# Four tiny reads on 15, 14, 8 and 7 DMA engines, late in a fused add and layer norm

## The chip, the cores and the metric

The kernel runs on one core of one Trainium2 chip. The metric is the device time of the run in microseconds (us). The kernel before takes 239.56 us (median of two runs, 239.42 to 239.70). Where a profile is quoted, the span on it (238.4 us) is a little shorter than the device time of the same run (239.69 us).

## The reference, cut to what matters

```python
# x, residual: 16 x 1024 x 512 float32; gamma, beta: 512
z = x + residual
mean = np.mean(z, axis=-1, keepdims=True)
var = np.var(z, axis=-1, keepdims=True)
z_norm = (z - mean) / np.sqrt(var + eps)
return (gamma * z_norm + beta).astype(np.float32)
```

That is 67.11 MB to read and 33.55 MB to write, with very little arithmetic for each byte.

## The kernel before

All large transfers are issued by SP, the sync engine, in one fixed order, and are carried out by 16 DMA engines (each large transfer has 16 landings in the trace). The trace does not number the engines. "Engine" with a number is a label of this document, for the order in which small transfers reach them: engine 15 is the one that 15 rows leave out. The general-purpose engine POOL adds, the scalar engine ACT makes the mean and the variance, the vector engine DVE normalizes in place in `zbuf`, and SP stores from `zbuf`. Each of the 128 partitions has room for 64 rows in `zbuf` and 32 in `rbuf`, so loads late in the list wait until a store has freed its rows. In this cut some lines of bookkeeping are left out, and the comments are added.

```python
X_CHUNKS = [8] * 15 + [4, 4]          # rows of a partition in each load
R_CHUNKS = [8] * 15 + [4, 4]
OUT_CHUNKS = [16] * 7 + [8, 4, 4]     # rows of a partition in each store
Z_ROWS, R_ROWS, STORE_LAG = 64, 32, 40
...
for c, (lo, n) in enumerate(loads_x):
    asked = lo + n
    while stored < asked - Z_ROWS:                     # room in zbuf?
        o = next(i for i, b in enumerate(stores) if b[0] == stored)
        nc.sync.wait_ge(so[o], 16)
        stored += stores[o][1]
    move(part(zbuf, Z_ROWS, lo, n), dram(xf, lo, n), sx[c])
    while todo_r and ...:
        wait_rows(s_add, "add", rlo + rn - R_ROWS)
        move(part(rbuf, R_ROWS, rlo, rn), dram(rf, rlo, rn), sr[rc])
    while todo_o and ...:
        wait_rows(s_out, "out", olo + on)
        move(dram(of, olo, on), part(zbuf, Z_ROWS, olo, on), so[oc])
for o, (lo, n) in enumerate(stores[:-1]):              # the end of the run
    if lo >= stored:
        nc.sync.wait_ge(so[o], 16)
nc.sync.sem_clear(range(nums[0], nums[-1]))
nc.sync.wait_ge(so[-1], 16)
```

Chunks are counted from 0 below. A load of 8 rows is 2 MB and puts 16 KB on each partition; a store of 16 rows is 4 MB and 32 KB.

## Time and profile before

| | before |
|---|---|
| device time | 239.56 us |
| transfers busy, share of 16 engines | 99.1% |
| ACT, DVE, POOL busy | 78%, 74%, 60% |
| last store landed | 238.33 us of a span of 238.4 us |

These are lines of the profile's page of the kernel before. The digits are busy tenths in 40 equal slices, and the line of queue 1 gives packets, MB and share of the time of 16 engines.

```profile
span 238.4 us, 1803 instructions
PE 3.7 (2%) x4; PEld 1.2 (0%) x4; DVE 177.2 (74%) x290; ACT 186.5 (78%) x545; POOL 142.2 (60%) x21
...
DMA  8999999999999999999999999999999999999996
...
DMA packets 6340, 100.67 MB, mean 422 GB/s; under 512 B 706, under 2 KB 706, under 8 KB 708
...
q1 hardware_dynamic: 6336, 100.67, 99.1%
...
ACT 38%; DMA 33%; issue 10%; POOL 7%; ACTq 5%; DVE 3%; SPq 1%; DVEq 0%; POOLq 0%
```

The transfers are full from the second slice to the last but one. The last line is the chain of waits; it runs through ACT for 38% of the span, but ACT is busy for only 78% of it, while the transfers have no idle slice. The reading is that the transfers bound this kernel.

The change is placed in the stretch around 142 us, so here are SP's issues there in the kernel before, from the timeline of SP (start, duration, what it issues).

```profile
141.22 0.43 SPq L138 DMA_DIRECT2D zbuf<-in_x_dram  x1
141.70 0.43 SPq L138 DMA_DIRECT2D rbuf<-in_residual_dram  x1
169.39 0.33 SPq L138 DMA_DIRECT2D zbuf<-in_x_dram  x1
```

SP issues x chunk 13 and residual chunk 13, and then x chunk 14 only 27 us later, when a store has freed rows. Meanwhile the engines work through what is queued. The end of the run shows in the waits of SP's own queue (line, what it waited for, total us, times, longest us):

```profile
SPq L166 <- DMA out_dram<-zbuf: 4.6, 2, 2.4
SPq L169 <- DMA out_dram<-zbuf: 2.3, 1, 2.3
```

These two lines are the wait for the stores after the last issue at 230.8 us.

One more reading is needed, and the page does not have it: the trace records when each of the up to 16 engines of a transfer reports that its part has landed. The following is worked out from those records of the kernel before; "late" is the last landing less the median one.

```
transfer            first     last      late
residual chunk 4     51.02     51.48    0.21
x chunk 9           114.39    115.25    0.63
residual chunk 13   177.74    179.14    1.13
last store          236.15    238.33    1.91
```

One landing falls behind the others, and only where stores run. It ends 1.5 us after the second last engine, so it alone sets the end of the run.

### The profile page before, as it was taken

Reading aid. Unit: us, or ns where it says so; the run is one execution under the profiler, and the core shown is the slowest. Engines: PE = TensorE matmul, PEld = TensorE weight load, DVE = VectorE, ACT = ScalarE, POOL = GpSimd, SP = SyncE. Lnnn points to the kernel's source line nnn. Section 1 sums busy time; section 2 is a strip of 40 time slices with the busy share of each in tenths; the row PEclk is TensorE's granted clock in tenths of the full one; section 3 lists DMA queues with packets and bytes.
Section 4 is the critical chain, followed back from the end, with each engine's and each line's share of the span. In section 5 each row is a group of like instructions: output and inputs, shape, how many; then the busy total and the mean of one; then the engine's idle time right before and its main releaser. Section 6 shows DMA issues by size and latency. Waiting matters only on the chain.

```text
span 238.4 us, 1803 instructions
## 1 busy us (share of the span) xinstructions
PE 3.7 (2%) x4; PEld 1.2 (0%) x4; DVE 177.2 (74%) x290; ACT 186.5 (78%) x545; POOL 142.2 (60%) x21
## 2 busy tenths in 40 slices
PE   0600000000000000000000000000000000000000
PEld 0100000000000000000000000000000000000000
DVE  0000488888888889998888888887888648888870
ACT  2003999999999999999999999989997399999700
POOL 0098988989889407893088930889209892770000
DMA  8999999999999999999999999999999999999996
GB/s 308 438 429 415 437 437 429 426 423 437 429 429 418 440 434 426 459 434 396 429 429 429 434 429 429 426 470 434 390 434 418 434 440 408 472 434 434 390 425 257
DMA packets 6340, 100.67 MB, mean 422 GB/s; under 512 B 706, under 2 KB 706, under 8 KB 708
## 3 DMA queue, kind: packets, MB, share of 16 engines
q1 hardware_dynamic: 6336, 100.67, 99.1%
q10 hardware_dynamic: 4, 0.00, 0.0%
HBM read 67.11 MB, written 33.55 MB: 422 GB/s over the span
## 4 chain that ended last, share of the span: by engine, by line
ACT 38%; DMA 33%; issue 10%; POOL 7%; ACTq 5%; DVE 3%; SPq 1%; DVEq 0%; POOLq 0%
DMA rbuf<-in_residual_dram 21%; ACT junk_s L203 20%; ACT junk_m L194 18%; DMA out_dram<-zbuf 12%; POOL zbuf L181 7%; ACTq L194 2%; DVE zbuf L228 2%; DVE zbuf L243 1%; ACTq L203 1%; SPq L138 1%; ACTq L189 1%; ACT std L211 0%; ACTq L201 0%; ACTq L210 0%; DVEq L228 0%
## 5 line engine op out<-in xcount | busy, mean ns | idle before, releaser
L181 POOL TENSOR_TENSOR zbuf<-zbuf,rbuf 128x4096 f32<-128x4096 f32 (+1 forms) x17 | 142.0, 8353 | 70.9 <-DMA rbuf<-in_residual_dram 70.9
L228 DVE SCALAR_TENSOR_TENSOR zbuf<-zbuf,nm,gamma_p 128x512 f32 x128 | 87.1, 743 | 50.4 <-ACT junk_s L203 50.4
L194 ACT ACTIVATE junk_m<-zbuf 128x512 f32 x128 | 74.9, 585 | 28.5 <-POOL zbuf L181 23.3
L203 ACT ACTIVATE junk_s<-zbuf,nm 128x512 f32 x128 | 88.8, 694 | 3.9
L243 DVE SCALAR_TENSOR_TENSOR zbuf<-zbuf,rstd,beta_p 128x512 f32 x128 | 87.1, 744 | 1.1
L203 ACT ACTIVATION_READ_ACCUMULATOR junk_s<-zbuf,nm x128 | 23.9, 187 | 0.0
L194 ACT ACTIVATION_READ_ACCUMULATOR junk_m<-zbuf x128 | 23.9, 187 | 0.0
L211 ACT ACTIVATE std<-ssq,eps_t x32 | 9.5, 297 | 3.7
L237 DVE RECIPROCAL rstd<-std x32 | 5.4, 170 | 0.0
L187 ACT ACT_TABLE_LOAD x1 | 1.3, 1283 | 2.7 <-PEq L55 2.7
L123 PE MATMUL gamma_p<-gb_row,ones 1*128 1x512 f32 x2 | 2.0, 1122 | 7.3 <-DMA gb_row<-in_gamma_dram 7.3
L123 PE MATMUL beta_p<-gb_row,ones 1*128 1x512 f32 x2 | 1.9, 1056 | 0.0
L118 DVE MEMSET ones<- 1x128 f32 x1 | 0.2, 165 | 2.0 <-PEq L55 2.0
L123 PEld LDWEIGHTS beta_p<-gb_row,ones 1*128 1x128 f32 x2 | 0.7, 332 | 1.0 <-DMA gb_row<-in_beta_dram 0.5
L123 PEld LDWEIGHTS gamma_p<-gb_row,ones 1*128 1x128 f32 x2 | 0.5, 305 | 7.3 <-issue 7.3
L278 POOL MEMSET const-float32-0.0<- 128x1 f32 x1 | 0.1, 99 | 0.2 <-issue 0.2
L278 POOL MEMSET const-bfloat16-1.0<- 128x1 bf16 x1 | 0.1, 101 | 0.0
L278 POOL MEMSET const-uint8-127<- 128x1 uint8 x1 | 0.1, 101 | 0.0
L278 POOL MEMSET const-float32-1.0<- 128x1 f32 x1 | 0.1, 98 | 0.0
L119 DVE MEMSET eps_t<- 128x1 f32 x1 | 0.1, 59 | 0.0
## 6 DMA issues: line engine op xcount, KB each, us to landing
zbuf<-in_x_dram SPq DMA_DIRECT2D x15, 2048.0 KB, 32.8
rbuf<-in_residual_dram SPq DMA_DIRECT2D x15, 2048.0 KB, 30.1
out_dram<-zbuf SPq DMA_DIRECT2D x7, 4096.0 KB, 28.6
zbuf<-in_x_dram SPq DMA_DIRECT2D x2, 1024.0 KB, 32.6
rbuf<-in_residual_dram SPq DMA_DIRECT2D x2, 1024.0 KB, 34.6
out_dram<-zbuf SPq DMA_DIRECT2D x1, 2048.0 KB, 15.0
out_dram<-zbuf SPq DMA_DIRECT2D x2, 1024.0 KB, 9.4
gb_row<-in_gamma_dram ACTq DMA_DIRECT2D x1, 2.0 KB
```

The costliest lines, as they stand in the source:

```text
L123: nc.tensor.matmul(dest[:, :], ones[:, :], gb_row[:, k * D : (k + 1) * D], start=True, stop=True).then_inc(s_pe, 1)
L138: i = nc.sync.dma_start(out=out, in_=in_).then_inc(s, 16)
L181: nc.gpsimd.tensor_tensor(out=z, in0=z, in1=part(rbuf, R_ROWS, a, an), op=ALU.add).then_inc(s_add, an)
L187: act.preload_act_table_set("sqrt_and_others")
L189: with act.Fori(0, turns) as t:
L194: act.activation(out=junk_m[k][:, :], in_=zbuf[:, bass.ds(zoff + k * D, D)], func=ACT.Identity, scale=-inv_d, accum_out=nm[:, bass.ds(r0 + ...
L203: act.activation(out=junk_s[k][:, :], in_=zbuf[:, bass.ds(zoff + k * D, D)], func=ACT.Square, bias=nm[:, bass.ds(r0 + k, 1)], accum_out=ss ...
L211: act.activation(out=std[:, bass.ds(r0, TURN)], in_=ssq[:, bass.ds(r0, TURN)], func=ACT.Sqrt, bias=eps_t[:, 0:1], scale=inv_d,).then_inc(s ...
L228: dve.scalar_tensor_tensor(out=row, in0=row, scalar=nm[:, bass.ds(r0 + k, 1)], in1=gamma_p[:, :], op0=ALU.add, op1=ALU.mult,)
L237: dve.reciprocal(out=rstd[:, bass.ds(r0, TURN)], in_=std[:, bass.ds(r0, TURN)]).then_inc(s_dve, TURN)
L243: dve.scalar_tensor_tensor(out=row, in0=row, scalar=rstd[:, bass.ds(r0 + k, 1)], in1=beta_p[:, :], op0=ALU.mult, op1=ALU.add,).then_inc(s_ ...
L278: nc = _bacc.Bacc("TRN2", target_bir_lowering=False, num_devices=1)
```

## The change

Four small reads are put on SP's queue just before the wait for x chunk 14. Nothing reads what they bring. They have 15, 14, 8 and 7 rows, of 64, 96, 128 and 160 bytes, and SP waits for them after all stores are issued. The sizes tell them apart in a trace, and the row counts tell engines apart: the intent is a label, not speed.

```diff
+PROBES = [(15, 16), (14, 24), (8, 32), (7, 40)]
...
+    probe = nc.alloc_sbuf_tensor("probe", [16, 128], FP32)
...
+    s_probe = [sem(f"probe{i}") for i in range(len(PROBES))]
...
     for c, (lo, n) in enumerate(loads_x):
         asked = lo + n
+        if c == len(loads_x) - 3:
+            at = 0
+            for i, (e, w) in enumerate(PROBES):
+                nc.sync.dma_start(out=probe[:e, at : at + w], in_=xf[:e, :w]).then_inc(
+                    s_probe[i], 16
+                )
+                at += w
         while stored < asked - Z_ROWS:
...
+    for s in s_probe:
+        nc.sync.wait_ge(s, 16)
     for o, (lo, n) in enumerate(stores[:-1]):
```

## The prediction

> **What bounds the kernel now.** The transfers. The DMA queue table gives queue 1 99.1% of sixteen engines' span (100.67 MB, mean 422 GB/s); ACT is busy 78%, DVE 74%, POOL 60%. The table by stages shows a DMA share of 0.99 to 1.02 from 20 us to 225 us. The chain of waits runs through ACT for long stretches, but it alternates with DMA there, and ACT has slack. So the time is bytes over rate, plus the tail: the last store lands at 238.3 us of a 238.4 us span.
>
> The landing times of each transfer, sixteen each, say more. Fifteen engines finish within about 0.6 us of each other; one falls behind. The spread from first to last landing grows from 0.45 us before the first store to 1.4 us at 179 us and 2.18 us at the end. It grows with the 4 MB stores, about 0.28 us each: that engine's 32 KB store packets take about 1,240 ns against 1,213 ns. This engine alone sets the end.
>
> **What the change does.** Four reads of 15x64 B, 14x96 B, 8x128 B and 7x160 B, issued before x chunk 14. Nothing else moves.[...] So engine 15 gets no probe, 14 one, 8 to 13 two, 7 three, 0 to 6 four. They look like labels that tell which engine lags.
>
> **Cost.**
> - Issue: 0.43 us each on SP's queue, as its neighbours, 1.9 us with gaps. They follow the residual issue at 141.70 us, and SP then waits for a store until 169.39 us. Off the path by 25 us.
> - Engines: a 4 B semaphore packet took 9 ns, a 2 KB packet 84 ns. I estimate 25 to 40 ns for a probe packet with its semaphore: at most 0.16 us on engines 0 to 6, 0.12 us on 7, 0 on 15. Fifteen engines have over 1.4 us of slack, so only what falls on the laggard counts.
> - Waits at the end: four satisfied semaphore waits, after the last issue at 230.8 us and under the last store's landing of 7.5 us. Zero.
> - 512 B more of SBUF per partition, four semaphores: zero.
>
> On the path: 0 if the laggard is engine 15, about 0.1 us if 7 or lower.[...] The trace before doesn't number the engines.[...]
>
> **Predicted time** 239.6 us; 239.1 to 240.2 should hold it 8 times in 10. Faster by over 2%: 0.01; within 2%: 0.98; slower by over 2%: 0.01.
>
> **What would show it.** The probes' issues appear at 142.1 to 144 us, about 0.43 us each, and x chunk 14 still issues at about 169.4 us. They land at 177.8 to 179.3 us, behind the residual chunk. If engine 15 lags, no probe has the landing that is late by about 1 us; if 7, the first three have it and the fourth not. 44 more data and 44 more semaphore packets. The last transfer's spread stays at 1.9 to 2.3 us. ACT, DVE, POOL busy times unchanged to 0.5%.
>
> **What would make it wrong.** A small descriptor that stalls the lagging engine[...]; a probe changing which engine is served first for the rest of the run; a transfer on fewer than 16 engines costing SP far more than 0.43 us; drift between runs over 0.3%.

The sum came to 239.6 us: 239.56 us of the kernel before, nothing for the issue, the waits and the space, and 0 or about 0.1 us for the probes on the lagging engine.

## The result, and the profile after

The changed kernel took 239.74 us (239.71 to 239.76, two runs) against 239.56 us. The ratio is 1.0009, with a 95% interval from 0.9985 to 1.0033. More rounds, on another occasion, are the first experiment below.

The same lines of the page, after:

```profile
span 238.4 us, 1809 instructions
PE 3.7 (2%) x4; PEld 1.2 (0%) x4; DVE 177.2 (74%) x290; ACT 186.5 (78%) x545; POOL 142.2 (60%) x21
...
DMA  8999999999999999999999999999999999999995
...
DMA packets 6428, 100.67 MB, mean 422 GB/s; under 512 B 794, under 2 KB 794, under 8 KB 796
...
q1 hardware_dynamic: 6424, 100.67, 99.1%
...
ACT 38%; DMA 33%; issue 10%; POOL 7%; ACTq 5%; DVE 3%; SPq 1%; DVEq 0%; POOLq 0%
```

The packets rise by 88: 15 + 14 + 8 + 7 = 44 rows and as many completions. (A completion is the packet of 4 bytes, of 9 ns, that goes with the landing of an engine's part of a transfer: there are 707 of them before and 751 after, 44 more for 44 more such landings.) The rest is the same. The issues of SP in the timeline, and its waits at the end:

```profile
141.16 0.43 SPq L143 DMA_DIRECT2D zbuf<-in_x_dram  x1
141.64 0.43 SPq L143 DMA_DIRECT2D rbuf<-in_residual_dram  x1
142.11 1.53 SPq L153 DMA_DIRECT2D probe<-in_x_dram  x4
169.33 0.36 SPq L143 DMA_DIRECT2D zbuf<-in_x_dram  x1
```

```profile
SPq L180 <- DMA out_dram<-zbuf: 4.6, 2, 2.4
SPq L183 <- DMA out_dram<-zbuf: 2.3, 1, 2.3
```

The four issues took 1.53 us in a gap of 27 us, x chunk 14 went out when it did before, and the added waits do not appear: the probes had landed 50 us earlier.

The landings of the four probes, worked out from the trace's records, are the interesting part. The first entry of each comes alone, 0.47 to 0.61 us after its issue, and no 4-byte packet goes with it (48 entries more than before, 44 packets more); the large transfers, with their 16 landings, have no such entry. What writes it was not shown. Then there is one for each row.

```
residual chunk 13   177.7 ... 178.2 178.3                                179.10
15 rows    142.7 |  177.9 ... 178.4 178.5                                179.31
14 rows    143.2 |  178.1 ... 178.6 178.7                                179.50
8 rows     143.5 |  178.3 178.4 178.5 178.6 178.6 178.6 178.9            179.68
7 rows     143.8 |  178.5 178.6 178.7 178.8 178.8 178.8                  179.88
```

That is 15, 14, 8 and 7 landings. The packets show which of the probes share an engine. In order of time the 44 packets fall into 15 series with steps of 13 to 16 ns, and each series starts with a packet of the first probe: seven have all four sizes, one has the first three, six the first two, and one the first alone. So the engines of a shorter probe are a part of those of a longer one, and the labels follow: engines 0 to 6 have all four probes, 7 has three, 8 to 13 have two, 14 has one and 15 none. (For fewer than seven rows it is taken for granted that the order goes on; there only the late engine was followed.) The late engine, which is in all four rows, is thus one of the engines 0 to 6. It is neither 15 nor 7.

The second thing to see is the spacing. The late engine ran its four probe packets in 0.06 us (178.61 to 178.67 us; 11 to 14 ns for each packet and 9 ns for each completion, overlapping a little). But their landings are 0.19 us apart, on this engine as on others. That is 0.77 us for four completions, twelve times the packets' time, and none of it reached the end of the run: the last store landed at 238.39 us, against 238.33.

### The profile page after: what moved, and what is told of

It is laid out like the page before. It is cut to its first block, busy times and chain, and to the rows that moved or that the text cites. A ratio compares the mean times of both kernels' runs of the same rounds, so it can differ in the third digit from the quotient of the medians.

```text
span 238.4 us, 1809 instructions
## 1 busy us (share of the span) xinstructions
PE 3.7 (2%) x4; PEld 1.2 (0%) x4; DVE 177.2 (74%) x290; ACT 186.5 (78%) x545; POOL 142.2 (60%) x21
## 4 chain that ended last, share of the span: by engine, by line
ACT 38%; DMA 33%; issue 10%; POOL 7%; ACTq 5%; DVE 3%; SPq 1%; DVEq 0%; POOLq 0%
DMA rbuf<-in_residual_dram 21%; ACT junk_s L217 20%; ACT junk_m L208 18%; DMA out_dram<-zbuf 12%; POOL zbuf L195 7%; ACTq L208 2%; DVE zbuf L242 2%; DVE zbuf L257 1%; ACTq L217 1%; SPq L143 1%; ACTq L203 1%; ACT std L225 0%; ACTq L215 0%; ACTq L224 0%; DVEq L242 0%
```

## The experiments

The rounds ran on three chips. Kernels of one call shared one chip and its runs of the kernel before, and every ratio is taken within such a call.

### The changed kernel again

Edit: none.

> The changed kernel itself, in more rounds. Theory (only what the probes add to the lagging engine counts; four probe packets with their semaphore packets took 0.06 us there): ratio 1.0003, between 0.9995 and 1.0012. Rival (the 0.18 us between the medians of the first two runs is a real cost, paid somewhere else than on the lagging engine): 1.0008 or more with an interval that leaves 1.0003 out. The lagging engine again lands last on all four probes if the lag belongs to one engine of the chip.

Measured: 239.65 us (239.55 to 239.67, five runs) against 239.65 us of before; ratio 0.9997, interval 0.9984 to 1.0011. What follows: the 0.18 us between the first medians is not a cost that can be told from nothing. The lagging engine was again in all four probes (its landings came at 179.12, 179.31, 179.50 and 179.70 us).

### Which engine lags

```diff
-PROBES = [(15, 16), (14, 24), (8, 32), (7, 40)]
+PROBES = [(6, 16), (5, 24), (4, 32), (3, 40), (2, 48), (1, 56)]
```

(The probe buffer was widened to fit.)

> Probes of 6, 5, 4, 3, 2 and 1 rows instead of 15, 14, 8 and 7, to find which of the engines 0 to 6 lags. If it is engine j, the probes of more than j rows have a landing about 0.8 us or more behind the others, and those of j rows or fewer have not. Time as before within 0.3%.

Measured: 239.76 us in one run of unknown state. The last landings:

```
6 rows: 179.35 (the one before it 178.3)      3 rows: 178.85
5 rows: 179.54 (the one before it 178.5)      2 rows: 179.04
4 rows: 178.69 (the one before it 178.7)      1 row:  179.22
```

What follows: the probes of 6 and 5 rows have a landing 1.0 us behind the others, and that of 4 rows has not. The lagging engine is the one that five rows reach and four do not, engine 4. Six small transfers on engine 0 and two on engine 4 cost nothing that shows.

### Twelve times as many

```diff
-PROBES = [(15, 16), (14, 24), (8, 32), (7, 40)]
+PROBES = [(15, 16), (14, 24), (8, 32), (7, 40)] * 12
```

(The destinations were spread over partitions so that they fit and do not overlap.)

> The four probes twelve times, 48 small transfers, issued in the same idle time of SP (about 20 us of issue from 142 us on, done before 169 us). Theory (a probe costs its packet times on the lagging engine and nothing else: 0.06 us for four): twelve times 0.06 = 0.7 us more, ratio 1.003 (1.002 to 1.004), and the lagging engine's distance to the median engine in the landing of the x chunk behind the probes not changed by more than 0.2 us, since the others carry nearly as many. Rival 1 (a small transfer stalls an engine[...], about 0.2 us each as the landings of the four are spaced): 48 x 0.2 = 9.6 us, ratio 1.04. Rival 2 (the cost is hidden altogether): 1.000.

Measured: 249.80 us; ratio 1.0416, interval 1.0402 to 1.0430, 10 us more. The first rival gave the right number. But two things happened in this run, as the timeline of SP and the stretches of the windows view show (in the latter: stretch, its length, busy us and instructions of PE, PEld, DVE, ACT and POOL, granted clock, DMA share, GB/s):

```profile
142.21 39.41 SPq L154 DMA_DIRECT2D probe<-in_x_dram  x48
181.67 0.36 SPq L143 DMA_DIRECT2D zbuf<-in_x_dram  x1
```

```profile
170.00:180.00 10.00, 0.00 (x0) 0.00 (x0) 8.67 (x15) 9.29 (x29) 0.47 (x1) 1.00 0.87 323
180.00:190.00 10.00, 0.00 (x0) 0.00 (x0) 8.26 (x13) 4.77 (x15) 8.38 (x1) 1.00 0.78 228
```

First, SP could not issue 48 transfers in 20 us. The first twelve went out within 4.5 us, and from then until about 176 us most took 1.2 us and four took 2.4 to 2.8, so x chunk 14 was issued at 181.67 us and not at 169.3. Even its first landing came 6.2 us later than before. Secondly, the engines lost unequal time: the last landing of x chunk 14 came 9.1 us later than before. So the match with 48 x 0.2 us was partly a coincidence, and the next kernels were made to separate the two.

### Waiting at once

```diff
                 at += w
+            for s in s_probe:
+                nc.sync.wait_ge(s, 16)
...
-    for s in s_probe:
-        nc.sync.wait_ge(s, 16)
```

> The same four probes, but SP waits for them directly after their issue, not at the end. Theory (the change is free because its wait stands behind the last issue): x chunk 14 is then issued at about 179.9 us, not 169.3 us, after the queue has run dry at 177.7 to 178.7 us; [...]an idle stretch of 3 to 4 us on every engine, and the time rises by 3 to 4 us, ratio 1.012 to 1.018. Rival (there is slack elsewhere that takes it up, since ACT and DVE have a backlog): within 0.3%.

Measured: 243.42 us; ratio 1.0152, interval 1.0136 to 1.0167, as expected. The wait of SP's queue, its timeline, and the DMA line of the view of transfers for 176 to 190 us (40 slices of 0.35 us):

```profile
SPq L158 <- DMA probe<-in_x_dram: 36.2, 1, 36.2
```

```profile
142.05 1.53 SPq L153 DMA_DIRECT2D probe<-in_x_dram  x4
179.92 0.36 SPq L143 DMA_DIRECT2D zbuf<-in_x_dram  x1
```

```profile
DMA  9995110000000093766898999979898996989999
```

What follows: x chunk 14 is issued 10.5 us later than before, and the queue runs dry for about 3.5 us. Data moves again in the slice from 180.9 us, 1.0 to 1.3 us after that issue. The change is free on SP's side because of where its waits stand. The slip of 10.5 us cost only 3.8 us, because the queue held most of the rest. While it was dry the late engine also caught up: at the end its landing is 0.80 us behind the median one, in place of 1.91.

### Sixteen in one burst

```diff
-PROBES = [(15, 16), (14, 24), (8, 32), (7, 40)]
+PROBES = [(15, 16), (14, 24), (8, 32), (7, 40)] * 4
```

> The four probes four times, 16 small transfers in one burst, issued by about 151 us, so that x chunk 14 is still issued at 169.4 us (in the run with 48 it slipped to 181.7 us, as SP's issue stretched to 1.2 us each after the 13th). Theory (an engine runs small packets at 16 ns each[...] and only their landings are spaced by 0.19 us): 16 x 0.016 = 0.25 us more, ratio 1.001. Rival (only about four can be outstanding, the others hold up the engine 0.19 us each): 12 x 0.19 = 2.3 us more, ratio 1.0095.

Measured: 242.58 us; ratio 1.0118, interval 1.0103 to 1.0134. The theory fell. The rival's 2.3 us were found on the lagging engine, but the interval leaves out its ratio of 1.0095. SP's timeline and the stretch from 177 to 182 us, first of this run and then, for comparison, of the kernel before:

```profile
142.09 9.34 SPq L154 DMA_DIRECT2D probe<-in_x_dram  x16
169.37 0.36 SPq L143 DMA_DIRECT2D zbuf<-in_x_dram  x1
...
177.00:182.00 5.00, 0.00 (x0) 0.00 (x0) 4.90 (x9) 4.70 (x14) 2.56 (x1) 1.00 1.04 318
```

```profile
177.00:182.00 5.00, 0.00 (x0) 0.00 (x0) 4.86 (x9) 4.69 (x14) 2.70 (x1) 1.00 1.00 426
```

Here x chunk 14 is issued on time, so SP is out of it. The DMA share still reads full, but only 318 GB/s move in place of 426. The busy share counts packets that are held up: behind the probes the trace has 16 KB packets of 0.7 to 2.4 us, where 0.61 is usual. From the last landing of residual chunk 13 to that of x chunk 14, the lagging engine took 7.18 us (179.29 to 186.47), against 4.89 us before (179.14 to 184.03). That is 2.29 us more, or twelve times 0.19 us. The first landing of x chunk 14 also came 0.46 us later, but that is another engine's: the landings that the probes of 15 and 14 rows lack put engines 15 and 14, with four probes or none, at about 178.2 us for residual chunk 13, and 4.89 us later is 183.1, where the first two landings stand (183.09 and 183.11). So those two were not slowed. At the end of the trace the last landing is 2.43 us later than before. Most of the rest of the measured 3.1 us lies outside the span that the profile shows: the device time exceeds the span by 1.8 us in all four runs of this kernel and by about 1.3 us in those of the others. Why was not found.

### Heavy reads on four engines or five

```diff
-PROBES = [(15, 16), (14, 24), (8, 32), (7, 40)]
+PROBES = [(4, 1024)] * 8          # the other kernel: (5, 1024)
...
+                    in_=xf[: 2 * e, :].rearrange("(p j) d -> p (j d)", j=2),
```

> Eight probes of four rows of 4 KB: about 0.165 us each, 1.3 us together, on engines 0 to 3 only. Theory (engine 4 alone sets the end, the others finish 1.5 us or more before it): ratio 1.000, within 0.0012; last landing of the run not moved. Rival (the mean load of the engines, or any engine's load, counts): 1.3 us, ratio 1.0055, or a part of it.

(The 0.165 us for a row is an estimate. In the trace before a packet of 2 KB takes 84 ns, one of 8 KB 309 ns and a completion 9 ns.)

Measured, four rows: 241.22 us; ratio 1.0071, interval 1.0058 to 1.0083.

> The same eight probes with five rows, so that engine 4, the lagging one, gets them as well. Theory: its 1.3 us go to the end in full, ratio 1.0055 (1.004 to 1.007), against 1.000 of the kernel with four rows. Rival (the lagging engine does not matter more than another): the same as with four rows, or a quarter more.

Measured, five rows: 242.92 us; ratio 1.0134, interval 1.0119 to 1.0149. The stretch of the run with four rows:

```profile
177.00:182.00 5.00, 0.00 (x0) 0.00 (x0) 4.96 (x9) 4.70 (x14) 1.47 (x1) 1.00 1.01 292
```

What follows: the first expectation missed. Only 292 GB/s moved in this stretch, more than half of its 16 KB packets took 0.7 to 1.25 us, and even the first landing of x chunk 14 came 1.5 us later than before. The heavy reads disturb engines that they do not use, so this pair is no clean test. All eight read the same 16 KB of x (20 KB with five rows), which may be the reason; that is argued and not shown. The difference of the two kernels, 0.0063 or 1.5 us, is near the 1.3 us expected for engine 4 alone. Each probe of five rows has one landing 1.8 to 2.7 us behind its next, those of four rows have none more than 0.36 us behind, so on this chip, too, engine 4 lags. A cleaner pair comes last.

### Stores in smaller pieces

```diff
-            move(dram(of, olo, on), part(zbuf, Z_ROWS, olo, on), so[oc])
+            for a in range(olo, olo + on, PIECE):          # PIECE = 8
+                an = min(PIECE, on)
+                move(dram(of, a, an), part(zbuf, Z_ROWS, a, an), so[oc])
```

(The waits for a store count 16 for each piece. This kernel has no probes.)

> No probes: the kernel before with every store cut into pieces of 8 rows, 16 KB per partition rather than 32 KB, issued at the same points. In the trace before, the lag of engine 4 grew by 0.25 us per 4 MB store with 32 KB packets and by 0.03 us in the 2 MB store with 16 KB packets. Theory (the lag comes with packets of 32 KB): the last landing is then 0.6 to 0.9 us behind the median one rather than 1.9, and the time falls by about 1.2 us, ratio 0.995. Rival (the lag comes with the bytes stored by this engine): lag and time unchanged, ratio 1.000 within 0.0015.

Measured: 240.06 us; ratio 1.0021, interval 1.0007 to 1.0034. The last store landed with its slowest engine 2.20 us behind the median one, against 1.91 before. What follows: the theory fell. The lag grew in small packets as in large ones, so shorter packets do not cure it; that it goes with the bytes stored fits, but was not tested by itself. Why engine 4 stores more slowly stays open.

### Twelve bursts of four

```diff
-        if c == len(loads_x) - 3:
+        if c >= 5:                       # four of the 48 probes before each chunk
+            for i, (e, w) in list(enumerate(PROBES))[4 * (c - 5) : 4 * (c - 4)]:
```

> The 48 small reads of the run at 249.8 us, but as twelve bursts of four, one before each of the last twelve x chunks, so that 5 us or more of ordinary transfers lie between two bursts. Theory (an engine's completions of small transfers land 0.19 us apart, but the engine runs up to about 0.8 us ahead of them, so a burst of four is hidden and each further one in the same burst costs 0.19 us): 12 x 0.06 = 0.7 us at most, ratio 1.000 to 1.004. Rival 1 (each small transfer costs 0.19 us wherever it stands, less the first four): 44 x 0.19 = 8.4 us, ratio 1.035. Rival 2 (a part of every burst shows): in between, 1.01 to 1.03.

Measured: 241.85 us; ratio 1.0090, interval 1.0076 to 1.0104. That is 2.2 us for 48 small transfers, where the single burst took 10.2 us. The theory expected at most 0.7 us, so the direction is right and the size is not: a burst costs about 0.18 us on average, not 0.06. In the trace the last landing is 2.16 us later than before at the end; 0.79 us of that came in one burst, at x chunk 12, and the other eleven cost 0.12 us each. Why that one was dearer was not found.

### Sixteen packets, two completions

```diff
-PROBES = [(15, 16), (14, 24), (8, 32), (7, 40)]
+PROBES = [(128, 16)] * 2
```

> Two reads of 128 rows of 64 B instead of sixteen reads of few rows: again sixteen small packets on an engine (on all 16 engines), but two completions in place of sixteen. Theory (the completions, one per transfer and engine, are what is slow): the two land 0.2 us apart and the cost is the packets' 16 x 16 ns = 0.25 us, ratio 1.001, at most 1.003. Rival (the small reads or writes themselves hold up the engine): 2.3 us or more, ratio 1.01, as sixteen reads cost.

Measured: 239.76 us; ratio 1.0007, interval 0.9994 to 1.0021. The same stretch:

```profile
177.00:182.00 5.00, 0.00 (x0) 0.00 (x0) 4.96 (x9) 4.70 (x15) 2.77 (x1) 1.00 1.04 419
```

What follows: sixteen small packets on every engine, the lagging one as well, cost nothing that shows when they belong to two transfers; the rate stays at 419 GB/s, and no 16 KB packet there took over 0.75 us. What cost 2.3 us was the number of transfers. (The two also use all 16 engines, which the sixteen did not; no run separates this.) Each transfer puts just one completion on each engine that it uses (44 packets of 4 bytes for the 44 rows of the four probes), so the runs cannot tell the completion from any other work done once for each transfer and engine. The landings spaced by 0.19 us point to the completion.

### Ten small reads, beside the lagging engine or on it

```diff
-PROBES = [(15, 16), (14, 24), (8, 32), (7, 40)]
+PROBES = [(4, 16)] * 10           # the other kernel: (5, 16)
...
+                rows = xf[1024 * i : 1024 * (i + 1), :].rearrange("(p j) d -> p j d", j=16)
-                nc.sync.dma_start(out=probe[:e, at : at + w], in_=xf[:e, :w])
+                nc.sync.dma_start(out=probe[:e, at : at + w], in_=rows[:e, 0, :w])
```

> Ten small reads of four rows, from rows spread over x, in one burst: (10 - 4) x 0.19 = 1.15 us on engines 0 to 3 only. In the heavy probes all rows came from the same few KB of x and every engine's packets slowed, which these avoid. Theory (engine 4 sets the end by 1.5 us, so this is hidden): ratio 1.000 to 1.001, last landing of engine 4 at its usual distance. Rival (a shared slowdown, or any engine's delay, counts): 1.15 us, ratio 1.005.

Measured, four rows: 239.51 us; ratio 0.9997, interval 0.9983 to 1.0010.

> The same ten with five rows, so that engine 4, the lagging one, gets them too. Theory: the 1.15 us go to the end in full, ratio 1.005 (1.003 to 1.006), and the lagging engine's distance to the median engine grows by about 1.1 us at the x chunk behind the probes and stays. Rival (no engine is special): the same ratio as with four rows. If both are 1.000, the sixteen reads were slow because they read the same addresses, not because of their completions.

Measured, five rows: 240.70 us; ratio 1.0046, interval 1.0032 to 1.0060. What follows: both expectations held. These are the landings of the three kernels, again worked out from the records:

```
                              before   four rows   five rows
residual chunk 13, last       179.14      179.24      178.85
x chunk 14, last              184.03      184.39      184.87
last store, second last       236.81      237.89      237.54
last store, last              238.33      238.46      239.18
```

The probes' landings tell which four or five engines they are on, and the others serve as the control. With four rows, twelve engines landed x chunk 14 about 4.89 us after residual chunk 13, within 0.02, engine 4 among them (184.12), and the four engines with probes about 1.0 us later than that. For the moment these four were last, by 0.27 us, but the time did not move, because by the end of the run engine 4 was last again, by 0.57 us. With a fifth row, eleven engines again took 4.89 us, within 0.02, and engine 4 took 6.01. Those 1.13 us went to the end: in the trace the last landing was 0.3 us earlier than before ahead of the burst, and 0.85 us later behind it and in the last store. One row of 64 bytes in each of ten transfers decides over 1.1 us. In the five-row probes the last landing is 0.70 us behind the one before it, in the four-row probes 0.04, so on this chip, too, engine 4 is the one that lags. SP's issue of x chunk 16 took 4.36 us in the run with five rows, in place of 0.43.

Put together, the burst on the lagging engine and what it added between those two landings:

| kernel | small packets on engine 4 | completions | added, us | (completions - 4) x 0.19 |
|---|---|---|---|---|
| changed kernel | 4 | 4 | 0.06 | 0 |
| five rows, ten times | 10 | 10 | 1.13 | 1.14 |
| the four, four times | 16 | 16 | 2.29 | 2.28 |
| two of 128 rows | 16 | 2 | 0.11 | 0 |

The last column is a rule that fits, not a mechanism that was seen, and its hundredths are not to be trusted: on engines 0 to 3 the same ten added 0.98 to 1.06 us, and twelve bursts of four cost 0.18 us each on average, where it says 0.

## Why the prediction was right or wrong

The time was right: 239.6 us predicted, 239.74 and then 239.65 measured, a ratio that cannot be told from 1. Point by point:

- **The transfers bound the kernel, and the last engine alone sets the end: right.** Ten small reads on engines 0 to 3 gave 0.9997, and the same with engine 4 gave 1.0046.
- **The issue is off the path: right.** Four issues took 1.53 us in a gap of 27 us, and x chunk 14 left at 169.33 us.
- **The waits cost nothing: right, for the reason given.** Moved up to the issue, the same waits cost 3.8 us.
- **Busy times, packet count and spread: right.** DVE, ACT and POOL are unchanged to 0.1 us, there are 88 more packets, and the last transfer's spread is 2.19 us (1.9 to 2.3 predicted).
- **Which engine lags: wrong.** The prediction reckoned with engine 15 or 7. The probes put the lag on an engine from 0 to 6; the first search gave engine 4 on one chip, and the pairs with four and five rows agree on two other chips. With engine 4 all four probes fall on the laggard, the dearest of the cases.
- **The cost of a probe: the term that was mis-sized.** "I estimate 25 to 40 ns for a probe packet with its semaphore" counted the engine's time for the packets. That is about 16 ns, even less. But a completion then lands only every 0.19 us, and this was not in the sum. Four of them take 0.77 us on the laggard, which would be 0.3% of the run. They did not show: with four the engine's landings came only 0.06 us later; by the runs with ten and sixteen, each further one in a burst costs about its 0.19 us (1.13 and 2.29 us). So the number came out partly by luck: the sum lacked a term that ten probes would have shown, and it happened to be asked about four. The prediction named a small descriptor that stalls the lagging engine as what could make it wrong. It was closer to that than its numbers tell: ten in place of four cost 0.46%.
- **Landings of the probes: nearly right.** 177.8 to 179.3 us predicted, 177.9 to 179.88 measured; the rest is the spacing of 0.19 us.

Left open are the reason why engine 4 stores more slowly, the dear burst among the twelve, the shared slowdown of the heavy reads, the 0.5 us outside the span with sixteen probes, and whether it is the completion itself that costs 0.19 us or other work done once for each transfer and engine. No version beat the kernel before. The lag of about 1.5 us behind the second last engine is about all that evening out the engines could gain (an estimate; no run tried it), and the small transfers of these runs could load engines 0 to 3 without engine 4 (four rows, ratio 0.9997), but no run loaded engines 5 to 15 without it.

## What to carry to other kernels

When transfers bound a kernel, ask which engine ends last, and cost a change on that engine alone; what falls on the others is free up to their distance from it, as the pair of four and five rows showed (0.9997 and 1.0046). Count small transfers by their number on an engine and not by their bytes: four in a row are nearly hidden here (0.06 us, and 0.18 on average over twelve bursts), more in one burst are not, and a few transfers of many rows are nearly free where many transfers of few rows are not (sixteen packets on engine 4 added 0.11 us as two transfers and 2.29 us as sixteen). Issue such extras where the issuing engine is idle, and wait for them only after the last issue that matters (the same waits, moved up, cost 3.8 us).
